# A decoder layer on one core: the statistic ahead of the up projection as one row from TensorE, with its root on ScalarE

## The chip, the cores and the metric

The kernel runs on one core of a Trainium2 chip. The metric is the device time of one execution in microseconds, as the median of several runs.

## The reference

One layer of a decoder, on 256 tokens of 2048 features in float32: a token mixer (mLSTM and RWKV-7 side by side), a cross-attention, and a channel mixer. Each of the three normalises its input, computes, normalises its output and adds it to the residual stream. The change lies between the second and the third:

```python
def rms_norm(x, g):
    xf = x.astype(jnp.float32)
    y = xf * lax.rsqrt(jnp.mean(xf * xf, axis=-1, keepdims=True) + RMS_EPS)
    return (y * g).astype(x.dtype)
...
def conv_glu_ffn(h, w_up, conv_w, conv_b, w_down):
    u = h @ w_up
    uc = conv_b + sum(conv_w[j] * shift_right(u, CONV_WIDTH - 1 - j) for j in range(CONV_WIDTH))
    gate, up = split_cols(uc, (D_FF, D_FF))
    return (jax.nn.gelu(gate, approximate=True) * up) @ w_down
...
        x = x + rms_norm(cross_attention(h, m, xattn_wq[l], xattn_wkv[l], xattn_wo[l]), xattn_post_norm[l])
        h = rms_norm(x, ffn_pre_norm[l])
        x = x + rms_norm(conv_glu_ffn(h, ffn_w_up[l], ffn_conv_w[l], ffn_conv_b[l], ffn_w_down[l]), ffn_post_norm[l])
```

The up projection has 2 x 8192 output features. The input statistic of the title is the root in `h = rms_norm(x, ffn_pre_norm[l])`, one number for each token.

## The kernel before, in words

**Layout.** Up to the down projection the activations stand with features on the 128 partitions and the 256 tokens along the row (kind "fm"). A number for each token is therefore wanted as a row of 256 that is the same on all partitions. The gain is put on before the product, the root behind it: the projection runs on x times gain, and the evacuation from PSUM multiplies by the row (`stf.rb`).

**Products.** Every float32 weight chunk is split in two: a rounded high part `wh` (a cast on ScalarE, L410) and the rest `wl` (a subtraction on VectorE, L431); the activations likewise. A product is then high x high, high x low and low x high. Weights come in chunks of 512 KB over the queue of SyncE (`Feed.dma`, L395). `raw` has 3 buffers, `wh` and `wl` have 4 each. While TensorE is given chunk i, `run` (L443) has chunk i+3 split and chunk i+6 loaded.

**Blocks.** The up projection takes up 64 gate columns and 64 up columns of 128 features. The first block is double (`two=True`, L1680): 16 chunks of 24 matmuls, in turn for its two groups of PSUM banks; a group holds two gate columns and two up columns. The next has 8 chunks of 24 matmuls and one group. From then on blocks are 256 columns, one gate and one up column: 4 chunks of 16 matmuls.

**Order of the work.** Everything on the five engines is issued in one order, written by `run`. Each chunk begins with a call of `side.half(True)` (a "front"), and has another `side.half()` at its middle. Each such half step may run pieces of side work, which are Python generators that yield between pieces:
- the evacuations of finished blocks wait in `bulk`, first in first out; one piece runs if the planner's credits for VectorE and ScalarE are both above 0. A half step adds 650 to VectorE's credit in the up projection (`RATE_D`) and 820 to ScalarE's, with a cap of 1200; a credit below -700 counts as -700 first. A VectorE instruction costs 130 + 1.04 for each element of a row, a ScalarE one 200 + 0.83 (`Meter`, L50). The casts and splits of weights are not charged.
- `chains` run one piece each time their gap of half steps has passed, if both credits are above -700.
- before a block starts, the evacuation of the block before the last one is run to its end (`side.need(pend[-2])`).

**The statistic.** `Residual` (L1309) adds the normalised output of the cross-attention to x and makes the two halves of x times gain, eight feature pairs in all, each as the product comes to need it. With the seventh pair it starts the chain `squares` (L1375): one pair's squares each half step, ScalarE squaring and VectorE adding into a [128, 2, 256] tile (`Stat.add`, L292). Then `finish(3)` (L364) follows: `fold` adds the tile's two halves; `column` (L323) multiplies by ones to get the sums with tokens on the partitions; `rstd_of` (L233) takes the root with a VectorE instruction and a power on GpSimd; `row` (L346) turns the column into a row on all partitions by two products with the identity; VectorE copies it from PSUM to `rb`. `column_of_sums` (L352) places the steps: fold, two yields, then yields until a front comes, column, three yields, row.

The first evacuation, `fu_evac(0)` (L1602), begins with `M["res"].wait(30)` (L1386): it yields until the chain has ended, at most 30 times. Each group then takes four pieces: us for the gate columns (VectorE, PSUM times row); the scaled base of the gate (ScalarE) and us for the up columns; the base of the up and two taps for each gate column (VectorE); Gelu (ScalarE) and the taps of the up; the product `ac`. In the same stage the chain `x_tokens` is started by this evacuation; it runs from 40 half steps later on, once every 6.

The same class has another way to a row, `rows` (L332), which the mixer's residual (`early`) uses for the statistic of the query projection: fold, yields, front, one product with ones that gives the sums as a row on all partitions, and `root` (L318): a logarithm and an exponential on ScalarE.

```python
        def rows(self, n, m):

            self.fold()
            for _ in range(n):
                yield
            while not side.front:
                yield
            q = aux("st", [P, S])
            mm(q, ones.broadcast_to((P, P)), self.parts[0])
            self.root(q)
            for _ in range(m):
                yield
            self.done = True
```

Of the kernel before, what the change touches and what calls it, by code (L numbers as in the profile page):

```python
# [152 lines left out]
def _layer(ctx, tc, nc, d, dbg):  # L153
# [1152 lines left out]
    def part(v, k2):  # L1306
        return v[k2 // 4][:, (k2 % 4) * 2:(k2 % 4) * 2 + 2]

    class Residual:  # L1309
# [65 lines left out]
        def squares(self):  # L1375
            for i in range(8):
                self.st2.add(part(M["xr"], i))
                if i < 7:
                    yield
            if self.early:  # L1380
                yield from self.st2.rows(6, 1)
            else:
                yield
                yield from self.st2.finish(3)

        def wait(self, n):  # L1386

# [352 lines left out]
    def fd_evac(n):  # L1740

        def gen(ps):
# [23 lines left out]
            if n == 0:  # L1766
                for g in range(4):
                    squares(g)
                    gain(g)
                    yield  # L1770
                return
            squares(0)
            gain(0)
            squares(1)
            finish(0)
            gain(1)
# [117 lines left out]
```

## Time and profile before

| | us |
|---|---|
| median of three runs | 1818.04 |
| the runs | 1817.80, 1818.04, 1819.45 |
| profiled execution, its own time | 1822.19 |
| span of its trace | 1820.4 |
| up projection in the trace, first matmul to last | 803 to 1480 |
| statistic of the up projection, first square to copied row | 831.7 to 852.6 |

The granted TensorE clock was 0.997 over the span. The profile is of one execution; engines are PE (TensorE matmul), PEld (its weight loads), DVE (VectorE), ACT (ScalarE), POOL (GpSimd) and SP (SyncE). An entry such as `us<-fm,stf_b` gives the tile written and the tiles read; `x4` is a count; brackets show how long the engine had been idle before and what ended the wait. The tiles of this statistic are `stf` (sums of squares), `st` (the product with ones), `var` and `stf_c` (the column and its root), `stb` (the row in PSUM) and `stf_b` (the row).

### The profile page before, as it was taken

Reading aid. Unit: us, or ns where it says so; the run is one execution under the profiler, and the core shown is the slowest. Engines: PE = TensorE matmul, PEld = TensorE weight load, DVE = VectorE, ACT = ScalarE, POOL = GpSimd, SP = SyncE. Lnnn points to the kernel's source line nnn. Section 1 sums busy time; section 2 is a strip of 40 time slices with the busy share of each in tenths; the row PEclk is TensorE's granted clock in tenths of the full one; section 3 lists DMA queues with packets and bytes.
Section 4 is the critical chain, followed back from the end, with each engine's and each line's share of the span. In section 5 each row is a group of like instructions: output and inputs, shape, how many; then the busy total and the mean of one; then the engine's idle time right before and its main releaser. Section 6 shows DMA issues by size and latency. Waiting matters only on the chain.

```text
span 1820.4 us, 30679 instructions
## 1 busy us (share of the span) xinstructions
PE 1802.0 (99%) x12054; PEld 1650.0 (91%) x12054; DVE 1341.2 (74%) x1937; ACT 1070.3 (59%) x1619; POOL 29.9 (2%) x52
## 2 busy tenths in 40 slices
PE   8999999999999999999999999999999999999998
PEld 8999988888888999899899999999999988888887
DVE  6879986666665757868888877878778776666665
ACT  6587445554554655666666667666556565555553
POOL 0100000000100000000000000000000000000000
PEclk9999999999999999999999999999999999999999
DMA  7655554354666765545566666666666666666664
GB/s 251 203 173 179 170 189 152 116 185 143 196 196 196 235 242 175 185 147 196 187 212 201 199 205 200 198 200 205 200 205 198 200 205 218 209 208 200 205 200 159
DMA packets 97889, 352.36 MB, mean 194 GB/s; under 512 B 11056, under 2 KB 11312, under 8 KB 97360
## 3 DMA queue, kind: packets, MB, share of 16 engines
q1 hardware_dynamic: 96496, 348.07, 59.7%
q8 instruction: 94, 1.54, 0.3%
q0 software_dynamic: 384, 1.18, 0.2%
q10 hardware_dynamic: 864, 1.15, 0.2%
q14 instruction: 51, 0.42, 0.1%
HBM read 347.73 MB, written 2.10 MB: 192 GB/s over the span
## 4 chain that ended last, share of the span: by engine, by line
PE 92%; DVE 4%; ACT 1%; issue 1%; DMA 1%; POOL 0%; DVEq 0%; POOLq 0%; SPq 0%; ACTq 0%
PE fm L189 51%; PE tm L189 37%; DVE wl L431 1%; DMA wsm<-in_w_sm_dram 1%; ACT wh L410 1%; PE gram L189 0%; PE Y L189 0%; DVE ql L66 0%; PE lv L189 0%; DVE tg L66 0%; DVE z L66 0%; PE X L189 0%; PE zwa L189 0%; PE num L189 0%; PE gramA L189 0%
## 5 line engine op out<-in xcount | busy, mean ns | idle before, releaser
L431 DVE TENSOR_TENSOR wl<-raw,wh 128x1024 fp32r<-128x1024 f32 x640 | 781.2, 1222 | 317.5 <-ACT wh L410 314.0
L410 ACT CAST wh<-raw 128x1024 fp32r<-128x1024 f32 x640 | 669.6, 1048 | 393.8 <-PE fm L189 172.1
L189 PE MATMUL fm<-fx,wh 128*128 128x512 f32 (+1 forms) x2240 | 673.1, 364 | 1.2 <-ACT fx L66 0.9
L189 PE MATMUL fm<-fx,wl 128*128 128x256 f32 x2048 | 559.2, 273 | 1.5 <-DVE wl L431 1.3
L189 PEld LDWEIGHTS fm<-fx,wh 128*128 128x128 f32 x2240 | 409.1, 190 | 50.3 <-ACT fx L66 1.1
L189 PEld LDWEIGHTS fm<-fx,wl 128*128 128x128 f32 x2048 | 393.2, 192 | 3.2 <-DVE wl L431 3.2
L189 PE MATMUL tm<-wh,as 128*128 128x512 f32 x1024 | 304.6, 379 | 0.0
L189 PE MATMUL tm<-wh,hx 128*128 128x512 f32 x768 | 232.0, 384 | 0.0
L189 PEld LDWEIGHTS tm<-wh,as 128*128 128x128 f32 x1024 | 193.5, 189 | 27.4
L189 PE MATMUL fm<-hx,wh 128*128 128x256 f32 x1120 | 193.6, 279 | 1.2 <-ACT wh L421 1.2
L189 PE MATMUL tm<-wl,as 128*128 128x512 f32 x512 | 194.0, 379 | 0.0
L189 PEld LDWEIGHTS fm<-hx,wh 128*128 128x128 f32 x1120 | 172.4, 194 | 2.6 <-ACT hx L66 1.4
L189 PEld LDWEIGHTS tm<-wh,hx 128*128 128x128 f32 x768 | 141.9, 189 | 19.5
L189 PE MATMUL fm<-hx,wl 128*128 128x256 f32 x560 | 155.5, 278 | 0.6 <-DVE wl L431 0.5
L189 PE MATMUL tm<-wl,hx 128*128 128x512 f32 x384 | 145.5, 379 | 0.0
L189 PEld LDWEIGHTS fm<-hx,wl 128*128 128x128 f32 x560 | 108.8, 194 | 1.0 <-DVE wl L431 0.7
L189 PEld LDWEIGHTS tm<-wl,as 128*128 128x128 f32 x512 | 96.8, 189 | 13.7
L66 ACT CAST as<-ac 128x256 fp32r<-128x256 f32 x128 | 45.5, 403 | 106.8 <-PE tm L189 106.8
L66 DVE TENSOR_TENSOR as<-ac,as 128x256 fp32r<-128x256 f32 x128 | 48.6, 421 | 55.6 <-ACT as L66 55.6
L66 ACT COPY ul<-fm 128x256 f32<-128x256 f32 x116 | 40.5, 373 | 73.2 <-PE fm L189 73.2
L189 PEld LDWEIGHTS tm<-wl,hx 128*128 128x128 f32 x384 | 72.6, 189 | 10.3
L189 PE MATMUL fm<-mgh,wh 128*128 128x256 f32 x256 | 70.7, 276 | 0.0
(361 smaller groups left out, 1954.5 us busy)
## 6 DMA issues: line engine op xcount, KB each, us to landing
raw<-in_w_fw_dram SPq DMA_DIRECT2D x232, 512.0 KB, 4.1
raw<-in_w_in_dram SPq DMA_DIRECT2D x160, 512.0 KB, 4.2
raw<-in_w_fd_dram SPq DMA_DIRECT2D x128, 512.0 KB, 3.7
raw<-in_w_br_dram SPq DMA_DIRECT2D x32, 512.0 KB, 4.1
raw<-in_w_mo_dram SPq DMA_DIRECT2D x32, 512.0 KB, 4.3
raw<-in_w_fu_dram SPq DMA_DIRECT2D x24, 512.0 KB, 3.5
raw<-in_w_xk_dram SPq DMA_DIRECT2D x8, 512.0 KB, 3.3
raw<-in_w_xq_dram SPq DMA_DIRECT2D x8, 512.0 KB, 3.3
```

The source lines that it names most:

```text
L66: return f(out, *a, **k)
L189: pe.matmul(out, lhsT, rhs, start=start, stop=stop, skip_group_check=True)
L410: nc.scalar.copy(wh, r)
L431: nc.vector.tensor_sub(wl, r, self.st[self.nl][0])
```

## The change

The residual ahead of the up projection ends its squares with `rows` instead of `finish`, as the mixer's residual does, with 2 yields ahead of the product and 1 after it. The yield that stood ahead of `finish` goes too. `rows`, `fold` and `root` are as before.

```diff
                 self.st2.add(part(M["xr"], i))
                 if i < 7:
                     yield
-            if self.early:
-                yield from self.st2.rows(6, 1)
-            else:
-                yield
-                yield from self.st2.finish(3)
+            yield from self.st2.rows(6 if self.early else 2, 1)
```

## The prediction

> **What bounds the kernel now.** I read the page first, then the table of windows over the up projection, the list of waits in the stretch that stood out, and last the timelines of the engines around the statistic.
>
> ```profile
> span 1820.4 us, 30679 instructions
> ...
> PE 1802.0 (99%) x12054; PEld 1650.0 (91%) x12054; DVE 1341.2 (74%) x1937; ACT 1070.3 (59%) x1619; POOL 29.9 (2%) x52
> ```
>
> TensorE is the bound, so an edit is worth only the TensorE instructions it removes and the TensorE stalls it ends. The question is whether this statistic causes a stall. The windows (columns: length, then busy time and count for each engine) show where one is.
>
> ```profile
> core 0: us, PE busy (x) PEld busy (x) DVE busy (x) ACT busy (x) POOL busy (x), PEclk, DMA share, GB/s
> 847.00:869.00 22.00, 22.00 (x198) 22.00 (x199) 14.34 (x22) 11.87 (x17) 0.70 (x1) 1.00 0.52 167
> 869.00:890.00 21.00, 19.82 (x115) 16.99 (x114) 18.79 (x32) 11.72 (x21) 0.00 (x0) 1.00 0.48 154
> 890.00:911.00 21.00, 20.61 (x125) 18.72 (x125) 19.05 (x30) 14.50 (x22) 0.00 (x0) 1.00 0.71 218
> 911.00:932.00 21.00, 21.00 (x130) 19.30 (x129) 19.38 (x29) 13.39 (x21) 0.00 (x0) 1.00 0.68 212
> ```
>
> From 869 on the blocks are 256 columns wide, and TensorE should run 130 matmuls in 21 us, as it does from 911. It runs 115, then 125. Twenty matmuls at 21/130 = 0.1615 us are 3.2 us lost. The busy column would say less: 1.18 + 0.39 = 1.57 us idle. The two differ because a matmul that waits a little still overlaps the end of the one ahead; the weight loads lose 19.30 - 16.99 = 2.31 and 19.30 - 18.72 = 0.58, together 2.89 us of load time, and 2.89 x 21/19.30 = 3.1 us of clock time. I take 3.2. The Trainium skill, page "Perfetto Trace Analysis", section "Identifying the Most-Contended Engine", says that matmul occupancy is no good measure because matmuls are pipelined, and that the busy share of weight loads should be read instead; by the column that it warns of, the stall would be worth 1.6 us and the whole change 2.0, by the one it prefers 3.1 and 3.5, and the matmul counts side with the second.
>
> ```profile
> PEld fm L189 <- DVE wl L431: 2.8, 5, 1.1
> ...
> PEld fm L189 <- ACT wh L410: 0.5, 1, 0.5
> ```
>
> Those are the waits of TensorE's weight loads from 869 to 904: it waits for weights that VectorE (low part) and ScalarE (high part) have not split yet. Why VectorE is behind there, and only there, is the point of this prediction.
>
> ```profile
> 841.84 1.48 DVE L66 TENSOR_TENSOR stf<-stf,sq 128x512 f32<-128x512 f32 x2
> 843.23 1.22 DVE L431 TENSOR_TENSOR wl<-raw,wh 128x1024 fp32r<-128x1024 f32 x1
> 844.37 0.42 DVE L66 TENSOR_TENSOR stf<-stf 128x256 f32<-128x256 f32 x1
> ...
> 847.33 0.16 DVE L66 TENSOR_SCALAR var<-st 128x2 f32<-128x2 f32 x1 [0.90 <-PE st L189]
> ...
> 852.15 0.42 DVE L66 COPY stf_b<-stb 128x256 f32<-128x256 f32 x1
> 854.13 1.23 DVE L431 TENSOR_TENSOR wl<-raw,wh 128x1024 fp32r<-128x1024 f32 x1 [1.57 <-ACT wh L410]
> 855.27 1.28 DVE L66 TENSOR_TENSOR us<-fm,stf_b 128x512 f32<-128x512 f32 x2
> ...
> 859.20 1.91 DVE L66 SCALAR_TENSOR_TENSOR tg<-us,cv,tg 128x255 f32<-128x255 f32 x4
> 861.02 1.91 DVE L66 SCALAR_TENSOR_TENSOR tu<-us,cv,tu 128x255 f32<-128x255 f32 x4
> ...
> 864.41 0.75 DVE L66 TENSOR_TENSOR ac<-tg,tu 128x256 f32<-128x256 f32 x2
> ...
> 874.99 0.75 DVE L66 TENSOR_TENSOR ac<-tg,tu 128x256 f32<-128x256 f32 x2
> 875.66 1.22 DVE L431 TENSOR_TENSOR wl<-raw,wh 128x1024 fp32r<-128x1024 f32 x1
> 876.80 1.28 DVE L66 TENSOR_TENSOR us<-fm,stf_b 128x512 f32<-128x512 f32 x2
> ```
>
> ```profile
> 844.12 1.05 ACT L410 CAST wh<-raw 128x1024 fp32r<-128x1024 f32 x1 [1.63 <-PE fm L189]
> 846.80 1.04 ACT L410 CAST wh<-raw 128x1024 fp32r<-128x1024 f32 x1 [1.63 <-PE fm L189]
> 849.93 1.05 ACT L410 CAST wh<-raw 128x1024 fp32r<-128x1024 f32 x1 [2.08 <-PE fm L189]
> 853.05 1.05 ACT L410 CAST wh<-raw 128x1024 fp32r<-128x1024 f32 x1 [2.08 <-PE fm L189]
> ...
> 860.27 1.28 ACT L66 ACT_TABLE_LOAD   x1 [1.25 <-DVE tg L66]
> 861.57 0.73 ACT L66 ACTIVATE tg<-tg 128x256 f32<-128x256 f32 x2
> ```
>
> Number the up projection's weight chunks from 0: the double block is 0 to 15, the next block 16 to 23, and the blocks of 256 columns follow from 24 (four chunks each). With four buffers the cast for chunk i+3 can only start when TensorE ends chunk i-1, so these casts date TensorE: chunk 15 starts at 844.1, 16 at 846.8, 17 at 849.9, 18 at 853.05. The double block is thus finished at 846.8, but its evacuation (us) starts at 855.27: its generator waits for the statistic. The row is copied at 852.15, half way through chunk 17, the statistic's generator ends at the start of 18, and the evacuation takes its first step half way through 18. Each of its two groups costs VectorE 1.28 + 1.91 + 1.91 + 0.75 = 5.85 us. Started so late, the second group ends only at 875.7, inside the wide blocks, with the split for chunk 27 behind it and the next block's evacuation (876.80) behind that. TensorE has three chunks in hand and runs dry:
>
> ```profile
> 881.19 0.38 PE L189 MATMUL fm<-fx,wl 128*128 128x256 f32 x1 [0.78 <-DVE wl L431]
> ```
>
> **The change, part by part.** First the TensorE work. The chain of waits has what goes:
>
> ```profile
> 846.87 0.34 PE st L189 x4
> ...
> 851.34 0.45 PE stb L189 x4
> ```
>
> That is 0.79 us for the column and its way back into a row. What comes is one product with ones of 256 columns. The statistic before the query projection already uses it:
>
> ```profile
> 746.04 0.28 PE L189 MATMUL fm<-qh,wl 128*128 128x256 f32 x1
> ...
> 746.15 0.60 PE L189 MATMUL st<-stx,ones 128*128 128x256 f32 x2
> ```
>
> From the end of the matmul ahead (746.32) to its own end (746.75) are 0.43 us. So TensorE gains 0.79 - 0.43 = 0.36; one interruption less of the main product may add 0.1. I take 0.4 (from 0.36 to 0.46).
>
> Second, other engines. VectorE loses 0.16 + 0.42 us, GpSimd one power; both off the bound. ScalarE gets a logarithm and an exponential, priced by the same earlier statistic:
>
> ```profile
> 747.91 0.47 ACT L66 ACTIVATE stx_b<-st,mhalf 128x256 f32<-128x256 f32 x1
> ...
> 748.41 0.42 ACT L66 ACTIVATE stx_b<-stx_b 128x256 f32<-128x256 f32 x1
> ```
>
> Together 0.89 us. No function table is loaded for them: the only load in this stage is the Gelu's at 860.27, and the Gelu needs their result, so it stays behind them.
>
> Third, a new wait: ScalarE stands at the logarithm until TensorE has done the product, and the casts of weights are queued behind. The product comes at the start of chunk 15, 844.1, and ends near 844.6; logarithm and exponential end near 845.55. The cast for chunk 18 moves from 844.12 to 845.55, its low part from 846.4 to about 847.9 at the end. TensorE needs chunk 18 only near 852.5 (853.05 less the TensorE term). Hidden, with 4.6 us to spare.
>
> Fourth, the order, which is the real term. The old path yields once, folds half way through chunk 14, must wait for a chunk start and takes 16; then three half chunks, the row, one more. The new path folds in the same step as the last square, at the start of 14; two yields bring it to the start of 15, which is a chunk start, so the product goes there, one chunk earlier; one yield later, half way through 15, it is done. (The fold ends near 843.7, before TensorE arrives at 844.1.) So at the end of the double block nothing is left to wait for. The planner agrees: after the fold its VectorE credit is far below the floor of -700, and 650 per half chunk make -50, 600, and the cap of 1200 by the middle of 15; ScalarE's is 1200 again at the start of 16. The first evacuation step goes at the start of 16 instead of half way through 18: five half chunks, near 847.9 instead of 855.27.
>
> Written out from there with the durations above (split 1.14, group 5.85) and the planner's credits: first group's steps at 16, middle 16, 17, middle 17 and middle 18; second group at 19, middle 19, 20, 21 and 22. VectorE then has, in chunks 16 to 23, 8 x 1.14 + 2 x 5.85 = 20.8 us of work in some 21.3: full, but finished. The splits run up to 2.5 us behind their earliest time; the last product of the second group ends near 866.7 instead of 875.7. In the wide blocks the next evacuation (chunks 24 to 26) and the first 256-column ones push the splits to 2 to 4 us behind. A split may be 5.5 us behind: three chunks of 2.58 us (16 matmuls at 0.1615), 7.7, less the 2.2 of the cast (1.05) and the split (1.14) themselves. The least reserve that I find is about 2 us. So I take the whole 3.2 us as ended, with 1.6 as the poor end.
>
> The sum: 3.2 + 0.4 = 3.6 us. The profiled execution took 1822.19 us around its span of 1820.4, so 1818.6 and 1816.8; against the median of the runs, 1818.04, which is 4.15 lower, the same microseconds give 1814.4. Nothing after 911 gains: there TensorE already runs at its pace.
>
> **The rivals.** (a) Part of the stall stays. For it: VectorE is at 20.8 of 21.3 us in chunks 16 to 23 and the next evacuation follows at once with a full credit; against it the reserve of 2 us. With half the stall left the gain is 1.6 + 0.4 = 2.0, 1816.0. (b) The transfer of time is hidden anyway: something else (a PSUM bank, a split standing ahead) still holds the evacuation back, or the burst merely stalls TensorE earlier by as much. Only the TensorE term is left: 0.4, 1817.6. Against it: in the timeline nothing but the row stands between 846.8 and 855.27. (c) The change doesn't do what it says for the order: the product misses chunk 15 and goes at 16, done in the middle of 16, evacuation at 17. Three half chunks are gained of five; in proportion 1.9 + 0.4 = 2.3, 1815.7. (d) Slower: ScalarE's stand at the logarithm starves TensorE. It decides only if the cast for chunk 18 comes more than 4.6 us later than I put it; every microsecond beyond is one of TensorE. To come out slower by 0.2% it would have to eat the 3.6 us gain and 3.6 more, so be late by 4.6 + 7.2, about 12 us: 1821.7. The earlier statistic's pair of activations, 0.89 us, speaks against it.
>
> **How the numbers follow.** A measurement of this kernel can tell about 0.2%, 3.64 us, from no change, so faster begins below 1814.40, and my forecast of 1814.4 lies on that line. Forecast 0.68, rival (a) 0.15, (b) 0.10, (c) 0.04, (d) 0.03. The forecast's two terms reach from 3.1 + 0.36 = 3.46 to the waits in full (2.8 + 0.5) and the interruption's 0.1, 3.3 + 0.46 = 3.76; the line at 3.64 halves it, 0.35 beyond and 0.33 short. So faster 0.35; within 0.33 + 0.15 + 0.10 + 0.04 = 0.62; slower 0.03. The range goes down to 1813.6 (3.76 off, then the 0.24 by which the lowest run lies under the median, and as much again and a little) and up past rivals (c) and (a), 1815.7 and 1816.0, as far again toward (b): 1817.0. Left out are (b) and (d), 0.13, and the tails.
>
> **What would show it.** In the changed profile: one product of two records with ones at the start of the last chunk of the double block and no product with the identity for stf; logarithm and exponential on ScalarE near 844.6; us near 848 instead of 855.27; the Gelu's table load near 852; and in the windows from 869 to 911 close to 130 matmuls per 21 us. Windows that still show 115 and 125 would make the forecast wrong though the statistic came early; a us near 851 would be rival (c); a wait of TensorE for wh between 850 and 856 rival (d).

## The result and the profile after

The changed kernel takes 1814.68 us (median of 14 runs, 1814.08 to 1816.32) beside 1818.15 for the kernel before (14 runs, 1817.69 to 1819.94). The ratio is 0.9981, with a 95% interval from 0.9974 to 0.9989: a gain of 3.5 us, somewhere from 2.0 to 4.7. One execution of path_old_time below took 3817 us and one of the kernel before beside it 4856, far above all others, and they are in no median or ratio of this document.

The two traces can't be subtracted as wholes. Their spans are 1820.4 and 1812.4, 8.0 us apart, more than twice what the runs say. The views of the tile that holds a statistic's row in PSUM tell where the surplus comes from: the row of the very first statistic, before and after (the last two times are the first and the last start).

```profile
L189 PE MATMUL stb<-con,st_c x4: 275/275/275, 39.0 to 39.3; 128*128 128x128 f32 x4
```

```profile
L189 PE MATMUL stb<-con,st_c x4: 275/275/276, 34.2 to 34.5; 128*128 128x128 f32 x4
```

By 39 us the profiled execution of before had lost 4.8 us, in code that the change doesn't touch. There TensorE stood 2.46 us for VectorE and then ran for 6.83 us at half its clock. The first line below shows the stand; the other two show the same two microseconds before and after, where the column after POOL is the granted clock.

```profile
31.18 0.97 PE L189 MATMUL st<-ones,st 128*128 128x1 f32 x4 [2.46 <-DVE st L66]
```

```profile
32.00:34.00 2.00, 2.00 (x10) 2.00 (x11) 0.34 (x2) 1.05 (x1) 0.70 (x1) 0.50 0.98 330
```

```profile
32.00:34.00 2.00, 2.00 (x21) 2.00 (x20) 1.21 (x1) 0.00 (x0) 0.00 (x0) 1.00 1.06 242
```

In the traces of the ten experiments below, whose opening is the same, this row comes between 34.3 and 35.3 seven times and at 37.0 to 37.5 three times. The three late ones show such a stand too, of 1.66 to 2.58 us, and half the clock after it; the seven others stood 1.45 us at most and kept the full clock. So a stage is compared with the same stage: from the first product of the up projection to the first of the down projection. Before, then after, in the views of the tiles `fx` and `as`:

```profile
L189 PE MATMUL fm<-fx,wh x2240: 275/382/483, 803.3 to 1479.7; 128*128 128x512 f32 x155, 128*128 128x256 f32 x32
...
L189 PE MATMUL tm<-wh,as x1024: 379/379/382, 1480.1 to 1811.1; 128*128 128x512 f32 x171
```

```profile
L189 PE MATMUL fm<-fx,wh x2240: 274/382/460, 798.3 to 1471.6; 128*128 128x512 f32 x155, 128*128 128x256 f32 x32
...
L189 PE MATMUL tm<-wh,as x1024: 378/379/382, 1472.0 to 1803.1; 128*128 128x512 f32 x171
```

To the hundredth the stage takes 676.79 us before and 673.63 after: 3.16 us less, which is most of the 3.5 of the medians and well inside their interval. Below, "the stage" is this time. It has two parts: the 24 chunks up to the blocks of 256 columns, 65.78 before and 65.79 after, and these blocks, 611.01 and 607.84. The whole gain lies in the second part. The windows of after, against those shown for before:

```profile
869.00:890.00 21.00, 21.00 (x131) 19.33 (x130) 18.91 (x32) 13.74 (x21) 0.00 (x0) 1.00 0.60 197
890.00:911.00 21.00, 21.00 (x131) 19.33 (x130) 17.89 (x28) 13.08 (x20) 0.00 (x0) 1.00 0.69 204
```

There are 131 matmuls in each, where there were 115 and 125, and 19.33 us of weight loads for 16.99 and 18.72: the stall is gone. The blocks of 256 columns begin at 869.0 before and at 864.1 after; the two times above, 611.01 and 607.84, count them whole. VectorE and ScalarE around the statistic, after:

```profile
837.41 1.48 DVE L66 TENSOR_TENSOR stf<-stf,sq 128x512 f32<-128x512 f32 x2
838.93 0.42 DVE L66 TENSOR_TENSOR stf<-stf 128x256 f32<-128x256 f32 x1
...
843.24 0.68 DVE L66 TENSOR_TENSOR us<-fm,stf_b 128x512 f32<-128x512 f32 x1
...
861.19 0.75 DVE L66 TENSOR_TENSOR ac<-tg,tu 128x256 f32<-128x256 f32 x2
```

```profile
840.21 0.48 ACT L66 ACTIVATE stf_b<-st,mhalf 128x256 f32<-128x256 f32 x1 [2.23 <-PE st L189]
840.71 0.42 ACT L66 ACTIVATE stf_b<-stf_b 128x256 f32<-128x256 f32 x1
841.04 1.03 ACT L410 CAST wh<-raw 128x1024 fp32r<-128x1024 f32 x1
...
847.78 1.28 ACT L66 ACT_TABLE_LOAD   x1
```

Counted from the first product of the up projection (798.33 here, 803.26 before), the first us starts at 44.9 instead of 52.0, and the second group's last product at 62.9 instead of 71.7. The cast of a weight chunk stands behind the logarithm, as forecast, and the Gelu's table load behind both. TensorE at the product:

```profile
838.99 0.28 PE L189 MATMUL fm<-fx,wl 128*128 128x256 f32 x1
839.50 0.67 PE L189 MATMUL st<-stf,ones 128*128 128x256 f32 x2 [0.23 <-DVE stf L66]
```

From the end of the matmul ahead (839.27) to the product's end (840.17) are 0.90 us, not 0.43. In this execution TensorE came before the fold had ended.

### The profile page after: what moved, and what is told of

Same layout as the page of the kernel before. It is cut to its first block, busy times and chain, and to the rows that moved or that the text cites. A ratio compares the mean times of both kernels' runs of the same rounds, so it can differ in the third digit from the quotient of the medians.

```text
span 1812.4 us, 30662 instructions
## 1 busy us (share of the span) xinstructions
PE 1798.7 (99%) x12048; PEld 1649.2 (91%) x12048; DVE 1340.1 (74%) x1935; ACT 1071.6 (59%) x1621; POOL 29.2 (2%) x51
## 3 DMA queue, kind: packets, MB, share of 16 engines
q10 hardware_dynamic: 864, 1.15, 0.2%
## 4 chain that ended last, share of the span: by engine, by line
PE 93%; DVE 3%; issue 1%; DMA 1%; ACT 1%; POOL 0%; DVEq 0%; POOLq 0%; SPq 0%; ACTq 0%
PE fm L189 52%; PE tm L189 37%; DVE wl L431 1%; DMA raw<-in_w_fu_dram 0%; PE gram L189 0%; PE Y L189 0%; DVE z L66 0%; DVE ql L66 0%; ACT wh L410 0%; PE lv L189 0%; PE X L189 0%; PE zwa L189 0%; DVE fx L66 0%; PE num L189 0%; PE gramA L189 0%
```

## The experiments

Two theories stood at first. Order: the statistic is ready earlier, so the evacuation of the double block starts earlier, and VectorE is not behind when the blocks of 256 columns begin. Path: the row by one product and two activations is itself the cheaper way, wherever it stands. The table has what was found; "chunks 0 to 23" and "loss in the wide blocks" are parts of the stage from each kernel's trace, the loss being what the blocks of 256 columns (the wide blocks) take over 607.84 us. Each stage is that of one execution.

| kernel | chunks 0 to 23 | loss in the wide blocks | stage | median, ratio to before (95%) |
|---|---|---|---|---|
| before | 65.78 | 3.17 | 676.79 | 1818.15; beside the experiments 1818.19, beside old_path_row16 1817.98 |
| after | 65.79 | 0 | 673.63 | 1814.68, 0.9981 (0.9974 to 0.9989) |
| late_evac5 | 65.36 | 2.88 | 676.08 | 1817.83, 0.9999 (0.9989 to 1.0008) |
| path_old_time | 65.32 | 2.91 | 676.06 | 1817.85, 0.9999 (0.9990 to 1.0008) |
| old_path_early | 67.58 | 0 | 675.42 | 1816.31, 0.9989 (0.9980 to 0.9998) |
| old_path_row16 | 66.02 | 0 | 673.86 | 1815.06, 0.9981 (0.9972 to 0.9990) |
| mid_product | 65.38 | 0 | 673.22 | 1814.71, 0.9980 (0.9972 to 0.9989) |
| late_evac2 | 65.39 | 0 | 673.23 | one execution, 1814.04 |
| late_evac4 | 65.34 | 0 | 673.18 | one execution, 1816.99 |
| late_no_taps | 65.71 | 0 | 673.55 | one execution, 1814.95 |
| act_hold24 | 73.96 | 0 | 681.80 | one execution, 1823.27 |
| act_hold12 | 67.20 | 0.29 | 675.33 | one execution, 1816.98 |

Single executions are read by their stage alone; that of late_evac4, for one, is one of the three with the late opening.

Seven of these kernels have the statistic of the change, with the product at the start of chunk 15: after, late_evac2, late_evac4, late_evac5, late_no_taps and the two act_hold. In their traces the fold ended between 40.37 and 41.02 us into the stage, while TensorE came to the product at 40.93 to 40.95. So it varied from one execution to the next whether TensorE waited there: from the end of the matmul ahead to the product's end are 0.80 to 0.90 us in after, late_no_taps and act_hold24, and 0.43 to 0.50 in the four others. In late_evac4:

```profile
842.28 0.28 PE L189 MATMUL fm<-fx,wl 128*128 128x256 f32 x1
842.39 0.60 PE L189 MATMUL st<-stf,ones 128*128 128x256 f32 x2
```

This alone can set the stages of two traces some 0.4 us apart: chunks 0 to 23 take 65.34 to 65.39 us in late_evac2, late_evac4 and late_evac5, and 65.79 and 65.71 in after and late_no_taps.

**The new statistic with the old start of the evacuation (late_evac5).**

```diff
                 yield from M["res"].wait(30)
+                for _ in range(5):
+                    yield
```

> The new statistic stays as it is, but the first evacuation of the up projection yields five half chunks after it is ready, so that it starts half way through chunk 18 as in the kernel before. Nothing of the computation changes. Theory (order): the gain is the earlier evacuation and nothing else, so the stall between chunk 24 and 32 is back, about 3.2 us over three blocks of 10.48 us, and the time is that of the kernel before, 1818.1 (within 0.5). Rival (the path itself: fewer instructions, no column, no power, no copy, is what gained): 1814.7 as with the change.

The ratio to before is 0.9999, and the windows show the stall again, nearly as large as it was (2.88 us for 3.17):

```profile
869.00:890.00 21.00, 19.68 (x113) 16.64 (x112) 19.13 (x34) 11.83 (x20) 0.00 (x0) 1.00 0.49 156
```

So the new path alone, with the evacuation as late as before, gains nothing that the runs can show.

**The new path at the old place (path_old_time).**

```diff
-            yield from self.st2.rows(6 if self.early else 2, 1)
+            if self.early:
+                yield from self.st2.rows(6, 1)
+            else:
+                yield
+                yield from self.st2.rows(2, 4)
```

> The row product and its root on ScalarE are kept, but placed where the old statistic stood: fold half way through chunk 14, product at the start of 16, end at the start of 18. Theory (order): the evacuation starts half way through 18 again, the stall of 3.2 us is back, and only TensorE's term is left: the product costs 0.4 against 0.9 for column and row, so 1817.7 (1817.2 to 1818.2). Rival (the path itself): 1814.7.

The same: 2.91 us of loss in the wide blocks, and no gain in the median. Chunks 0 to 23 take 65.32 for 65.78, 0.46 less: that is the TensorE term of the prediction, at its upper end, from one trace of each. The stage is 0.73 shorter, too little to see in the runs here.

**The old path at the new place (old_path_early, old_path_row16).** Column, power, products with the identity and copy, but early. The second makes the row half a chunk later, with `column_of_sums(2, 2, True)`.

```diff
+        def early_finish(self):
+            yield from self.column_of_sums(2, 1, True)
+            self.rb = cp.tile([P, S], F32, tag="strb", bufs=1, name=self.name + "_b")
+            dve.tensor_copy(self.rb, self.row())
...
-            yield from self.st2.rows(6 if self.early else 2, 1)
+            if self.early:
+                yield from self.st2.rows(6, 1)
+            else:
+                yield from self.st2.early_finish()
```

> The old path (column, power on GpSimd, two products with the identity, copy by VectorE) at the place of the new one: fold with the last square, column at the start of chunk 15, row half way through 15, evacuation at the start of 16. Theory (order): the stall stays away; TensorE has 0.45 more to do, so about 1815.1 (1814.6 to 1815.6), the wide blocks at 10.48 us each. Rival (the path itself): 1818.1, or in between if the row now has to wait for GpSimd.

The wide blocks lose nothing, as the order theory has it. But the median came out at 1816.31 and not at 1815.1, and the trace shows why, TensorE first, then GpSimd:

```profile
842.75 0.58 PE L189 MATMUL st<-ones,stf 128*128 128x1 f32 x4 [0.50 <-DVE stf L66]
...
845.54 0.71 PE L189 MATMUL stb<-con,stf_c 128*128 128x128 f32 x4 [0.78 <-POOL stf_c L236]
```

```profile
843.88 1.61 POOL L236 TENSOR_TENSOR stf_c<-var,mhalf 128x2 f32<-128x2 f32 x1 [138.68 <-DVE var L66]
```

TensorE is idle at the column (0.50, for the fold) and again at the row (0.78, for GpSimd's power, which took 1.61 us here and 0.70 in the kernel before). Counted by the steps between ends of matmuls that is 0.63 and 1.04 beyond the usual step. The first is the late fold of one execution once more: the second kernel has its column at the same place and didn't wait there. It moves the row out of the second wait.

> As old_path_early (column at the start of chunk 15, power on GpSimd, copy), but the row is made half a chunk later, at the start of 16, and the evacuation starts half way through 16. In old_path_early TensorE stood 1.04 us at the row because GpSimd had not ended, and 0.63 at the column because the fold had not. Theory: the root's path only matters by what TensorE stands at; with the row later GpSimd is done, the stand of 1.04 goes, the wide blocks stay at 10.48. Stage 673.2 + 0.45 for the second interruption, plus 0 to 0.6 for the fold: 673.7 to 674.3; time about 1815.0 (1814.4 to 1815.7). Rival (GpSimd's way is slow for another reason): stage 675 or more.

With the row half a chunk later the wait for GpSimd is gone, though the power took 1.70 us here. The stage is 673.86, and the ratio is that of the change. So the root on ScalarE is not needed for the gain. What it does is to let the row stand in one place close behind the squares, with no instruction of GpSimd on the way.

**The product half a chunk later (mid_product).** It may go at a chunk's middle, and the statistic ends there.

```diff
-        def rows(self, n, m):
+        def rows(self, n, m, front=True):
...
-            while not side.front:
+            while front and not side.front:
...
-            yield from self.st2.rows(6 if self.early else 2, 1)
+            yield from self.st2.rows(6 if self.early else 3, 1 if self.early else 0, self.early)
```

> As the change, but the product does not wait for a chunk's start: it goes half way through chunk 15, and the statistic ends there at once. The evacuation still starts at 16. In the changed kernel TensorE stood about 0.5 us at the product because the fold had not ended. Theory: that stand goes, the stage from the first product of the up projection to the first of the down projection falls from 673.63 to about 673.2, and the time to 1814.3 (1813.9 to 1814.7, hardly to be told from 1814.7 by time, only by the stage). Rival: the row comes too late for the first evacuation step, ScalarE's casts slip by half a chunk and part of the stall returns, 1815 to 1816.

```profile
841.05 0.28 PE L189 MATMUL fm<-fx,wl 128*128 128x256 f32 x1
841.17 0.60 PE L189 MATMUL st<-stf,ones 128*128 128x256 f32 x2
```

There is no wait, and 841.77 - 841.33 = 0.44 us from end to end. The stage is 673.22, 0.41 shorter than in the trace of the change. But that is not the place's doing: the fold ended 40.31 us into the stage here, so a product at the chunk's start would not have waited either, and late_evac2 and late_evac4, with the product at the start, have stages of 673.23 and 673.18. A later place leaves more room for a late fold; that it gains anything is not shown, and the medians, 1814.71 and 1814.68, are the same.

**How late is too late (late_evac2, late_evac4).** The edit of late_evac5 with 2 and 4 half chunks.

> As the change, with the first evacuation put off by two half chunks instead of five (start of chunk 17 instead of half way through 18). In late_evac5 the stall was back: 10.61, 12.89 and 10.82 us for the first three wide blocks, 2.9 us in all. If the loss is in proportion to the delay, 1.2 us; if it has a threshold (three chunks in hand, about 2 us of reserve), two half chunks or 2.7 us use up the reserve and 0 to 0.7 us are lost. Stage from the first product of the up projection to the first of the down projection 673.6 to 674.3 against 674.8.

> As late_evac2 with four half chunks (start of 18). In proportion 2.3 us lost; with a threshold near 2.7 us of delay, and one for one beyond it, 5.3 - 2.7 = 2.6 us. The dose of two half chunks tells the two apart, this one only bounds them.

Both theories of the dose fall. Two half chunks cost nothing, and four cost nothing either; the fifth brings 2.88 us. The reserve of each split (from its end to TensorE's start of that chunk) makes it plain. Its smallest value in chunks 16 to 43 is 2.85 us with the change, 2.79 with two half chunks of delay, 0.56 with four; with five it is used up, and TensorE is at the chunk ahead of its split five times (by 1.21 at chunk 28, then 0.40, 0.40, 0.64 and 0.40, together 3.05). From four to five the reserve falls by about 3.6 us, though a half chunk is 1.3. From the end of chunk 20's split to the end of chunk 28's VectorE has the same work in both kernels, but not the same idle time. Its waits there with four half chunks:

```profile
852.03 1.23 DVE L431 TENSOR_TENSOR wl<-raw,wh 128x1024 fp32r<-128x1024 f32 x1 [0.85 <-ACT wh L410]
...
855.95 1.23 DVE L431 TENSOR_TENSOR wl<-raw,wh 128x1024 fp32r<-128x1024 f32 x1 [0.27 <-ACT wh L410]
...
865.27 1.23 DVE L431 TENSOR_TENSOR wl<-raw,wh 128x1024 fp32r<-128x1024 f32 x1 [0.27 <-ACT wh L410]
...
874.03 1.23 DVE L431 TENSOR_TENSOR wl<-raw,wh 128x1024 fp32r<-128x1024 f32 x1 [1.56 <-ACT wh L410]
```

and with five:

```profile
849.70 1.23 DVE L431 TENSOR_TENSOR wl<-raw,wh 128x1024 fp32r<-128x1024 f32 x1 [1.45 <-ACT wh L410]
850.84 1.28 DVE L66 TENSOR_TENSOR us<-fm,stf_b 128x512 f32<-128x512 f32 x2
853.62 1.23 DVE L431 TENSOR_TENSOR wl<-raw,wh 128x1024 fp32r<-128x1024 f32 x1 [1.50 <-ACT wh L410]
...
858.83 1.22 DVE L431 TENSOR_TENSOR wl<-raw,wh 128x1024 fp32r<-128x1024 f32 x1 [0.32 <-ACT wh L410]
...
864.62 1.23 DVE L431 TENSOR_TENSOR wl<-raw,wh 128x1024 fp32r<-128x1024 f32 x1 [1.56 <-ACT wh L410]
...
875.20 1.23 DVE L431 TENSOR_TENSOR wl<-raw,wh 128x1024 fp32r<-128x1024 f32 x1 [1.55 <-ACT wh L410]
```

These waits add up to 2.95 us against 6.38, and the 3.4 us of difference are nearly the whole 3.6. Begun in the middle of a chunk, the first us stands behind a split that VectorE spends 1.45 us waiting for; then two us products stand together (x2), the base on ScalarE waits for the first of them, and the cast of the next chunk is queued behind the base. ScalarE with five half chunks:

```profile
851.56 1.09 ACT L66 ACTIVATE tg<-us,cv 128x256 f32<-128x256 f32 x2 [1.89 <-DVE us L66]
852.56 1.03 ACT L410 CAST wh<-raw 128x1024 fp32r<-128x1024 f32 x1
```

Begun at a chunk's start, the us runs while the cast does. The kernel before also began in the middle of a chunk, with the fifth half step.

That the place in the chunk is the cause is read from these rows; no kernel changed it alone, and three half chunks weren't tried. Another pair bears on it. The first us of old_path_row16, in the middle of chunk 16, starts 46.45 us into the stage and has the second us right behind it; that of late_evac2, at the start of 17, starts at 46.26 and stands alone. The evacuation of the double block ends at 68.06 in the one and at 65.89 in the other, and the smallest reserve is 1.25 us for 2.79. The two differ in the path of the statistic as well.

**VectorE's work taken out (late_no_taps).** late_evac5, and in `taps`:

```diff
             def taps(i):
+                if b < 2:
+                    dve.spent += 2 * (130.0 + 1.04 * 255) + 2 * (130.0 + 1.04 * 254)
+                    return
```

> As late_evac5, but the evacuations of the double block leave out the convolution's taps (16 instructions of VectorE, 2 x 2 x 1.91 = 7.6 us); the planner is charged for them as before, so that the order stays. Theory (the stall is VectorE's late work piled up in the wide blocks): the wide blocks run at 10.48 us although the evacuation starts as late. Rival (the late evacuation frees PSUM banks late, or ScalarE's part of it is what stalls): 12.9 us in the second wide block as in late_evac5, or nearly.

```profile
869.00:890.00 21.00, 21.00 (x130) 19.30 (x129) 18.65 (x31) 14.01 (x23) 0.00 (x0) 1.00 0.62 196
```

The evacuation starts as late as in late_evac5 (51.9 us into the stage for 51.6) and has read the last bank of the double block's first group as late (53.2 for 52.9), that of the second 0.9 us earlier. Yet there is no stall, and the smallest reserve is 1.14 us. In the trace of late_evac5, too, each wait of TensorE in the first 100 us of the stage was ended by a split or a cast and none by a us. So the load of VectorE is what the late start pushes into the wide blocks, and TensorE doesn't wait for the PSUM banks.

**ScalarE held up (act_hold24, act_hold12).**

```diff
             self.root(q)
+            if n == 2:
+                for _ in range(24):
+                    nc.scalar.copy(self.acc[:, 1], self.acc[:, 1])
```

> As the change, with 24 copies of 256 elements on ScalarE (about 0.33 us each, 8 us in all) right behind the exponential, so that the cast for chunk 18 waits 8 us longer. The prediction's rival (d) put the reserve of that cast at 4.6 us: TensorE should then stand about 3.4 us at chunk 18, between 850 and 857, and more if the evacuation, late on ScalarE too, brings the stall in the wide blocks back (up to 3.2). Stage 677 to 680. If there were no such reserve, 8 us and more: over 681.

ScalarE and then TensorE:

```profile
841.94 10.44 ACT L344 COPY stf<-stf 128x256 f32<-128x256 f32 x24
852.29 1.99 ACT L413 CAST wh<-raw 128x1024 fp32r<-128x1024 f32 x2
```

```profile
853.38 0.76 PE L189 MATMUL fm<-fx,wh 128*128 128x256 f32 x2 [4.27 <-ACT wh L413]
854.64 0.58 PE L189 MATMUL fm<-fx,wl 128*128 128x256 f32 x1 [0.51 <-DVE wl L434]
```

The copies were longer than I had put them, 10.44 us in all. TensorE stood 4.70 + 0.97 = 5.67 us beyond the usual steps, so about 4.8 of the hold were covered (the split of chunk 18 has a reserve of 4.72 in the trace after); the prediction had 4.6. But the stage grew by 8.2 us, not 5.7. The windows give the rest:

```profile
855.00:858.00 3.00, 3.00 (x15) 3.00 (x15) 2.96 (x6) 2.14 (x5) 0.00 (x0) 0.50 0.78 195
...
861.00:864.00 3.00, 3.00 (x29) 3.00 (x28) 2.96 (x7) 1.90 (x3) 0.00 (x0) 1.00 0.53 180
```

After the idle time TensorE ran at a granted clock of 0.50 up to about 860, 15 matmuls in 3 us instead of 29. That is the other 2.5 us.

> As act_hold24 with 12 copies. Twenty-four took 10.44 us, 0.435 each, and TensorE stood 4.70 + 0.97 = 5.67 us, so that the reserve was about 4.7. Twelve take 5.2: TensorE stands about 0.5 us at chunk 18, stage about 674.1, and nothing more if half the hold only costs what lies beyond the reserve. Rival (the loss is in proportion): half of 8.2, about 4 us, stage 677.7.

Neither fitted: the stage is 675.33. TensorE stood 0.32 us at chunk 18, less than expected, but with ScalarE 5.2 us behind, later splits were late as well: 0.30 and 0.29 us at chunks 20 and 21, 0.97 at chunk 23 and 0.29 in the first wide block, 2.2 us in all. The reserve of 4.7 us holds for that one cast; the work behind it has less.

## Why the prediction was right, point by point

The time was forecast as 1814.4 and is 1814.68. The ratio of 0.9981 lies beside the line of 0.2%, as forecast, and its interval reaches to both sides of it. The larger of the two terms, the stall, and what ends it came as forecast; the smaller was missing in the profiled execution, and a fit to 0.3 us is closer than a sum can promise whose smaller term comes and goes by 0.4.

- **The stall is the statistic's doing.** Shown. Forecast were 3.2 us, by the counts of matmuls; 3.17 us is what the wide blocks gained, and a late evacuation alone brings 2.88 back. The busy column, 1.6, would have been half of it, and the weight loads' 3.1 were right. The Trainium skill, page "Perfetto Trace Analysis", section "Identifying the Most-Contended Engine", prefers the loads' busy share to that of the matmuls, and these traces agree.
- **TensorE's term, 0.4 us.** Its size is right: path_old_time has 0.46, mid_product 0.40 (65.78 - 65.38), and late_evac2, late_evac4 and late_evac5 0.39 to 0.44. In the trace of the change it is nought, because there the fold was not done when TensorE came. I had it end at 843.7 for an arrival at 844.1, on the clock of the trace before; in the trace after, with 4.93 taken off, it should have ended at 838.8 and ended at 839.35. The end of the fold moved by 0.65 us among the seven executions above, so a margin of 0.4 us was too thin to lean on.
- **The order.** The product came at the start of chunk 15, us at the start of 16. VectorE was busy for 20.6 of the 21.4 us of chunks 16 to 23, for 20.8 of 21.3 forecast, and the smallest reserve of a split, put at about 2 us, is 2.85.
- **ScalarE's new wait is hidden.** Shown; the split for chunk 18 ends 4.7 us ahead of TensorE.
- **The rivals.** (a) and (b) are out: nothing of the stall is left, and the evacuation starts when the row is there. (c) did not come about, and its price was wrong: it is a delay of two half chunks, and late_evac2 loses nothing by that. (d) had its deciding point right for the one cast and its slope wrong. A hold of 5.2 us cost about 2 us and not 0.5, because later splits had less reserve; one of 10.4 cost 8.2 and not 5.7, because the clock was halved after a wait of more than 4 us.
- **Profile and median.** The profiled execution stood 4.15 us over the median. That was one late opening, 4.8 us lost before 40 us, and nothing near the change.

3.16 us are accounted for by the stage. The medians say 3.5. The 0.3 between lies inside the interval; executions with the fold done in time, with a stage near 673.2, could supply it, but how many of the runs were such is not known.

## What to carry to other kernels

An edit to a small statistic is worth what is waiting for its result: look for the generator, evacuation or load that stands behind it, and for the reserve that its lateness uses up later, some 25 us on in this case (from the first us at 52.0 us into the stage to the first wait at 76.7). Price a delay by that reserve and not in proportion: four half chunks cost nothing and the fifth cost 2.9 us. And compare traces stage by stage, for two executions can differ by 5 us before the edited code begins.

## What the runs showed of the hardware

- In act_hold24, after 4.27 us without a matmul, TensorE was granted half its clock for about 7 us (0.50 from 854 to 860, then 1.00); after 0.78 us, in the kernel before, it was not. In the opening of the kernel shorter stands did the same: after 1.66, 2.42, 2.46 and 2.58 us (old_path_early, old_path_row16, before, late_evac4) the clock was 0.50 for 3.4 us or, before, 6.8 us. After six stands of 0.54 to 1.45 us there it stayed at 1.00. The Trainium skill, page "TensorE: Matmul & The Clock Gate", section "HAM oscillation — how this bites in real kernels", warns of gaps of TensorE over some 3.4 us. The gap of 4.27 us agrees; the four between 1.66 and 2.58 us lie under that figure and halved the clock all the same, and here the measurement decides.
- GpSimd's power on 128 x 2 elements took 0.70 us in the kernel before and 1.61 and 1.70 in the two kernels with the old path early, where a split of weights ran on VectorE during 1.05 and 1.15 us of it (843.72 to 844.93 in old_path_early). In the kernel before a split overlapped it by 0.38 us. Whether that is the reason wasn't tried.
- A copy of 256 elements on ScalarE from SBUF to SBUF, in place, took 10.44/24 = 0.435 us, one behind the other.
